# A two-layer hybrid decoder trunk on one core: a new order of the paired output tiles, and new limits in the emission planner

## The chip, the cores and the metric

The kernel runs on one core of a Trainium2 chip. The metric is device time in microseconds (us) of one execution; lower is better. Engines are named as in the profile: PE is TensorE's matmul and PEld its weight load, DVE is VectorE, ACT is ScalarE, POOL is GpSimd, SP is SyncE, which issues most of the DMAs. L468 is line 468 of the kernel before. "Tile" alone means a weight tile.

## The reference

One inference step of two layers, for 256 prompt tokens and 8 single-token samples (264 columns in all, model width 1024), all in float32:

```
x = LN(a*x + 0.5*swiglu(x))                      # FFN 0, inner width 2048
x = LN(a*x + mix(x) @ wo)
x = LN(a*x + 0.5*swiglu(x))                      # FFN 1
x = LN(a*x + sigmoid(x @ pe_gate) * (p @ pe_proj))

mix = sigmoid(m1)*(norm(o_ret)*silu(rg)) @ w_ret_out      # retention, 4 heads
    + sigmoid(m2)*(rms(o_ssm*silu(z)) * nw) @ w_ssm_out   # SSD, 16 heads, rms over 2 groups of 512
    + sigmoid(m3)*(rms(o_gdn)*nw*silu(gz)) @ w_gdn_out    # gated delta rule, 8 heads
```

Each of the three branches is a linear recurrence with a state per head. For the prompt it is computed in chunks from a zero state; the gated delta rule needs the inverse of a unit triangular 64x64 matrix per chunk and head. For each of the 8 samples one step is taken from a given state, 512 KB for each branch, sample and layer, and the updated state is written back: 48 states are updated.

## The kernel before

**Dense products.** Activations are stored transposed, 128 channels by 264 columns, as a high and a low part (`xh`, `xl`) whose sum is the float32 value; weights are split in the same way while they stream in. A weight tile is 128x1024 numbers, 512 KB. SP fetches it into `raw`, ACT copies it to the high part `whi` (L444), DVE subtracts to get the low part `wlo` (L344), and PE makes 24 matmuls of it (L468): 8 hi·xh, 8 hi·xl, 8 lo·xh. There are 239 such tiles in each layer, in a fixed order: 48 of FFN 0, 125 of the mix's inputs and branch outputs with the branches' gates between them, 8 of `wo`, 48 of FFN 1, 2 of `pe_proj`, 8 of `pe_gate`. In the mix the order is: inputs for retention (`ret`), SSD (`ssm`), `rg`; then the 8 output tiles `ro` of retention with the gate tiles `m1`; `gq`, `gv`, `mz`; SSD's output `so` with `m2`; `gz`; the delta rule's output `go` with `m3`; `wo`. The program line for DVE instructions is always L344, for ACT L444, for ACT with a running sum L442, for ACT's table loads L450, for PE L468 and its transposes L473, since a helper records them; they are told apart by their tiles.

**Prefetch.** `stream(upto)` (L562) emits the DMA and the ACT copy of the tiles up to a number; `stream_lo()` (L582) emits the DVE subtractions still owed. High and low parts live in a ring of 3; further ones, and all states and scratch of the branches, share 29 slots.

**The planner.** Emission order is set by the program itself, which keeps an estimated clock for each engine (class `Clocks`). Recurrences, sample readouts and state updates are generators ("tasks"): between weight tiles `pump()` (L668) lets a task emit its next step if the task's inputs are ready by the estimated clocks and ACT and DVE are less than a limit behind PE (`slack`, L662). A step that yields 1 was marked `easy` (L659) and may be emitted even when they are further behind; only the inverse of the triangular matrix (31 steps of two DVE instructions on `t<-inv,ub` and `ub<-ub,t`) yields 1. `drain()` (L701) and `force()` (L682) run tasks to their end at once, where their result is needed. `Clocks.dma` (L318) books a DMA at 358 bytes per ns plus a lag of 950 ns, after which what was loaded counts as ready. The state updates (`updates`) issue a state's load only if the estimated DMA queue ends before PE's clock plus a limit: `SPARE` (500) where no other task is left, `SPARE2` (-500) otherwise.

**Branch outputs.** For each of `ro`, `so`, `go`, `wo` the first two tiles are done as a pair (`two`, L745), because the branch's result `y` (split in `yh`, `yl`) comes late: first inner tiles 0 to 6 for both, then inner tile 7. The gate tiles before them (`rg`, `mz`, `gz`) multiply into the branch result one by one if its recurrence is done, or else are kept in slots (`z`) and multiplied together in `finish()` (L1361), which also drains the tasks. For SSD the function `mz` (L1375) also squares the product (ACT) and hands a closure `sq` to `late` (L1406): `DSQ` tiles later PE adds the square up with a matmul against ones, and after the eighth DVE scales and splits the result for `so`.

Of the kernel before, what the change touches and what calls it, by code (L numbers as in the profile page):

```python
# [12 lines left out]
AF = mybir.ActivationFunctionType  # L13
# [6 lines left out]
NB = 8  # L20
# [28 lines left out]
MORE_F = 4  # L49
MORE_ROOM = 0  # L50
AHEAD = 3
SPARE = 500.0
SPARE2 = -500.0
BACKLOG = 3000.0
BACKLOG_0 = 3000.0
BACKLOG_1 = 6000.0
LEAD2 = 4
HOLD = 2
DSQ = 1
NJ = 7  # L60
NN = 4
NS = 2
# [1 line left out]
UROOM = 5  # L64
UROOM_F = 4
# [168 lines left out]
class Clocks:  # L234
# [83 lines left out]
    def dma(self, key, out, in_, counts=True):  # L318
        n = 4.0
        for d in out.shape:  # L320
            n *= d
        t = self.run(key, 450.0 if key == "SP" else 1200.0, [out], [in_], False)
        t = self.at["DMA"] = max(self.at["DMA"], t) + n / 358.0
        self.note("DMA", t + 950.0, [(self.region(in_), False), (self.region(out), True)], counts)
        return t + 950.0


class Eng:
# [19 lines left out]
class Trunk:  # L348
    def __init__(self, ctx, tc, io, depth):
        self.tc, self.nc, self.io, self.depth = tc, tc.nc, io, depth  # L350
        nc = self.nc
        self.ck = Clocks()
        self.at = self.ck.at
        self.V = Eng(self, "DVE", nc.vector, 70.0, 1.05)
        self.G = Eng(self, "POOL", nc.gpsimd, 300.0, 1.55)
        self.SY = Eng(self, "SP", nc.sync, 0.0, 0.0)
        self.PE = nc.tensor
        self.ready = {}
        self.cp = ctx.enter_context(tc.tile_pool(name="cp", bufs=1))
        self.wp = ctx.enter_context(tc.tile_pool(name="wp", bufs=1))  # L360
        self.bp = ctx.enter_context(tc.tile_pool(name="bp", bufs=1))
        self.sp = ctx.enter_context(tc.tile_pool(name="sp", bufs=1))
        self.mp = ctx.enter_context(tc.tile_pool(name="mp", bufs=4, space=bass.MemoryType.PSUM))
        self.pp = ctx.enter_context(tc.tile_pool(name="pp", bufs=4, space=bass.MemoryType.PSUM))
        self.uid = 0
        self.live = 0
        self.freed = [0.0] * NSLOT
        self.peak = 0
        self.banks = 4
        self.aset = None  # L370
        self.tasks = []
        self.prio = {}
        self.easy = {}
        self.late = []
        self.total = depth * NCH
        self.wpos = self.fpos = 0
        self.raw = {}
        self.x = []
        self.wt = {}
        self.half = []  # L380
        self.more, self.ramp, self.wring, self.wslots = 0, None, [], {}
        self.res = RES
        self.hold = False
        self.ln_s = None
        self.xf = None
        self.keep = False
        self.unbiased = {}
# [261 lines left out]
    def step(self, t):  # L649

        self.ck.last = 0.0
        self.ready_at = max(self.at["PE"], self.at["DVE"])
        try:
            r = next(t)
        except StopIteration:
            self.tasks.remove(t)
            return True
        self.ready[t] = 0.0 if r == 2 else self.ck.last - (3000.0 if r else 0.0)
        self.easy[t] = r == 1  # L659
        return r != 0  # L660

    def slack(self, t):  # L662
# [5 lines left out]
    def pump(self):  # L668

        stuck = set()  # L670
        while True:
            behind = max(self.at["ACT"], self.at["DVE"]) - self.at["PE"]
            for t in self.tasks:
                if t not in stuck and self.ready.get(t, 0.0) <= self.at["PE"] and \
                        (behind < self.slack(t) or self.easy.get(t)):
                    break
            else:
                break
            if not self.step(t):
                stuck.add(t)  # L680
# [63 lines left out]

    def two(self, idx, xs):  # L745

        self.stream(idx + 3)
        self.use(idx + 1)
        ps = [self.mmtile()[:, :T] for _ in range(2)]
        for js in (range(7), (7,)):  # L750
            for j in js:
                for g in range(2):
                    for k in range(2):
                        self.mm(ps[g], self.wt[idx + g][k][:, j, :], xs[j][0], start=j == 0 and k == 0, stop=False)
            for j in js:
                for g in range(2):
                    self.mm(ps[g], self.wt[idx + g][0][:, j, :], xs[j][1], start=False, stop=j == 7)
        for g in range(2):
            self.used(idx + g)
        self.stream(idx + 4)  # L760
        return ps
# [303 lines left out]
    def pe_gate(self, idx, final):  # L1065
        wait, last = [], []

        def product(m, t):
            p = self.t4(self.prj[m // 4])[:, m % 4, :]
            self.stt(p, t, 1.0, p, ADD, MUL)  # L1070
            wait.append((m, p))

        def gate(m, ps, b, sc):
            t = self.t264()
            self.act(t, ps, AF.Tanh, scale=0.5 * sc, bias=b)
            if m == MORE_P:
                self.ramp = 0
            if m == 7:
                self.table(AF.Ln)
            if last:  # L1080
                product(*last.pop())
            last.append((m, t))
            if m == 7:
                product(*last.pop())
            if m == ALG_P:
                self.ln_begin(3, final, False)
            while m >= ALG_P and wait:
                ks = wait[:GN]
                del wait[:GN]
                for k, q in ks:  # L1090
                    self.resid(k, q)
                self.ln_add(*ks, delay=GD)
                if m < 7:
                    break
        idx = self.run(idx, 8, self.x, gate, 2, ALG_P, lambda i: True)
        self.free(*self.prj)
        self.drop()
        return idx
# [39 lines left out]
    def mix(self, idx, prev):  # L1138
        nc, V, G = self.nc, self.V, self.G
        l = self.l  # L1140
# [286 lines left out]
        convs = 28  # L1427
        for g, i in MIX[13:]:
            out = {"m2": "so", "m3": "go"}.get(g, g) if i >= LEAD2 - 2 else g
            if out in end and out not in src:  # L1430
                src[out] = end[out]()
            if g == "wo" and i == 0:
                self.free(*mixed)
                self.ln_begin(1)
                self.ramp = MORE_W
            xs = ym if g == "wo" else src[g][0] if g in src else self.x
            if i < 2 and g in ("ro", "so", "go", "wo"):
                if i == 0:
                    for e, ps in enumerate(self.two(idx, xs)):
                        do[g](e, ps)  # L1440
                        self.after()
                        self.pump()
                    idx += 2
                continue
            idx = self.run(idx, 1, xs, lambda _, ps, *a: do[g](i, ps, *a))
            convs -= g in ("ssm", "gq", "gv")
            if convs == 0:
                self.store(self.io["cso"][l], cs.rearrange("p t b -> p (t b)"), self.G)
                convs = -1
# [206 lines left out]
    def updates(self, l, todo):  # L1656

        for kind in range(3):
            while kind not in todo:
                yield 0  # L1660
            rows, decay, update = todo[kind]
            q, n = [], 0
            while n < NB or q:
                did = False
                for e in q:
                    b, S, R, k, t = e
                    if self.at["PE"] < t or self.hold and k < 2:
                        continue
                    if k == 2:
                        self.store(self.io["sts"][l, kind, b], S[0][:, 0:1024])  # L1670
                        self.free(S[0])
                        q.remove(e)
                    elif k == 1:
                        update(b, S[0], R[0])
                        self.free(R[0])
                        e[3:] = 2, self.ck.last
                    else:
                        decay(b, S[0])
                        e[3:] = 1, max(self.ck.last, R[1])
                    did = True  # L1680
                    break
                if not did and n < NB and not self.hold and self.room((UROOM_F if len(self.tasks) == 1 else UROOM) - self.res) and self.idle_dma(SPARE if len(self.tasks) == 1 else SPARE2):
                    S, R = self.ld_state(l, kind, n), self.ld_row(rows, n)
                    q.append([n, S, R, 0, S[1]])
                    n += 1
                    did = True
                yield (2 if did else 0)
# [824 lines left out]
```

## Time and profile before

| | before |
|---|---|
| runs of the kernel before | 1784.69, 1784.53, 1779.51 us (median 1784.53) |
| the profiled execution's own time | 1778.85 us |
| its span | 1777.1 us |
| mean granted TensorE clock | 0.984 of full speed |
| PE busy | 1679.2 us, 94% |
| DVE busy | 1300.5 us, 73% |
| ACT busy | 1033.8 us, 58% |
| data moved | 373.14 MB, 210 GB/s on average |

The span runs from the first to the last instruction; the execution's own time has 1.8 us more around it. Busy shares are averages over stages; the idle time of PE is read place by place in the timelines, with the engine that released it. "PEclk" is the granted TensorE clock, 1.0 for 2.4 GHz and 0.5 for 1.2 GHz. A matmul starts while the one before it drains, so busy times of single matmuls overlap.

### The profile page before, as it was taken

Reading aid. Unit: us, or ns where it says so; the run is one execution under the profiler, and the core shown is the slowest. Engines: PE = TensorE matmul, PEld = TensorE weight load, DVE = VectorE, ACT = ScalarE, POOL = GpSimd, SP = SyncE. Lnnn points to the kernel's source line nnn. Section 1 sums busy time; section 2 is a strip of 40 time slices with the busy share of each in tenths; the row PEclk is TensorE's granted clock in tenths of the full one; section 3 lists DMA queues with packets and bytes.
Section 4 is the critical chain, followed back from the end, with each engine's and each line's share of the span. In section 5 each row is a group of like instructions: output and inputs, shape, how many; then the busy total and the mean of one; then the engine's idle time right before and its main releaser. Section 6 shows DMA issues by size and latency. Waiting matters only on the chain.

```text
span 1777.1 us, 35137 instructions
## 1 busy us (share of the span) xinstructions
PE 1679.2 (94%) x14026; PEld 1592.1 (90%) x14026; DVE 1300.5 (73%) x2554; ACT 1033.8 (58%) x1918; POOL 58.6 (3%) x60
## 2 busy tenths in 40 slices
PE   8999999899989999999899999998999899999997
PEld 8999998779889898999799999987798898989996
DVE  5566858958767788777875678598586677887767
ACT  5455665347754345676764556654477544457766
POOL 0000011000000100000000000100000000000000
PEclk9999999899999999999999999998999999999999
DMA  9663557387537885598446635573774378846871
GB/s 322 179 204 125 162 193 261 107 279 243 159 101 255 313 278 195 204 337 283 151 128 183 209 123 166 200 247 115 254 253 145 114 269 321 278 158 240 324 275 45
DMA packets 129492, 373.14 MB, mean 210 GB/s; under 512 B 24032, under 2 KB 40544, under 8 KB 129328
## 3 DMA queue, kind: packets, MB, share of 16 engines
q1 hardware_dynamic: 127664, 365.13, 61.2%
q0 software_dynamic: 1664, 5.77, 0.8%
q8 instruction: 110, 1.80, 0.4%
q14 instruction: 54, 0.44, 0.1%
HBM read 334.73 MB, written 36.12 MB: 209 GB/s over the span
## 4 chain that ended last, share of the span: by engine, by line
PE 58%; DVE 22%; ACT 11%; DMA 5%; issue 3%; SPq 0%; ACTq 0%; DVEq 0%
PE mm L468 49%; PE b L468 8%; DVE wlo L344 8%; DMA S<-sti 4%; ACT whi L444 3%; DVE t L344 2%; DVE y L344 2%; ACT L450 2%; DVE S L344 2%; ACT t L444 2%; PE b L473 1%; DVE xl L344 1%; DMA raw<-w 1%; DVE gk L344 1%; DVE gv L344 1%
## 5 line engine op out<-in xcount | busy, mean ns | idle before, releaser
L444 ACT ACTIVATE whi<-raw 128x1024 fp32r<-128x1024 f32 x478 | 502.2, 1056 | 398.5 <-PE mm L468 277.2
L468 PE MATMUL mm<-xh,whi 128*128 128x264 f32 x2464 | 627.3, 290 | 16.9 <-ACT xh L444 7.6
L344 DVE TENSOR_TENSOR wlo<-raw,whi 128x1024 fp32r<-128x1024 f32 x478 | 577.8, 1219 | 67.8 <-ACT whi L444 66.7
L468 PE MATMUL mm<-xl,whi 128*128 128x264 f32 x2464 | 618.1, 286 | 2.6 <-DVE xl L344 2.3
L468 PEld LDWEIGHTS mm<-xh,whi 128*128 128x128 f32 x2464 | 466.3, 189 | 32.8 <-issue 12.5
L468 PEld LDWEIGHTS mm<-xl,whi 128*128 128x128 f32 x2464 | 466.3, 189 | 6.6 <-DVE xl L344 4.1
L468 PE MATMUL mm<-xh,wlo 128*128 128x264 f32 x2464 | 351.3, 285 | 6.6 <-DVE wlo L344 6.5
L468 PEld LDWEIGHTS mm<-xh,wlo 128*128 128x128 f32 x2464 | 320.7, 189 | 8.7 <-DVE wlo L344 8.4
L468 PE MATMUL mm<-yh,whi 128*128 128x264 f32 x512 | 136.6, 299 | 4.8 <-ACT yh L444 4.8
L468 PE MATMUL mm<-hh,whi 128*128 128x264 f32 x512 | 128.4, 287 | 0.0
L468 PE MATMUL mm<-hl,whi 128*128 128x264 f32 x512 | 127.1, 284 | 0.0
L468 PE MATMUL mm<-yl,whi 128*128 128x264 f32 x512 | 113.5, 284 | 0.0
L468 PEld LDWEIGHTS mm<-yh,whi 128*128 128x128 f32 x512 | 101.4, 198 | 10.8 <-ACT yh L444 6.2
L468 PE MATMUL mm<-yh,wlo 128*128 128x264 f32 x512 | 93.7, 295 | 14.7 <-DVE wlo L344 14.7
L468 PEld LDWEIGHTS mm<-hh,whi 128*128 128x128 f32 x512 | 96.4, 188 | 5.1 <-issue 5.1
L468 PEld LDWEIGHTS mm<-hl,whi 128*128 128x128 f32 x512 | 96.4, 188 | 0.0
L468 PEld LDWEIGHTS mm<-yh,wlo 128*128 128x128 f32 x512 | 79.2, 198 | 16.3 <-DVE wlo L344 16.3
L468 PEld LDWEIGHTS mm<-yl,whi 128*128 128x128 f32 x512 | 88.9, 188 | 0.0
L468 PE MATMUL mm<-gh,whi 128*128 128x266 f32 x304 | 82.3, 292 | 0.0
L468 PE MATMUL mm<-gl,whi 128*128 128x266 f32 x304 | 80.4, 286 | 0.0
L468 PE MATMUL mm<-hh,wlo 128*128 128x264 f32 x512 | 72.6, 284 | 0.9 <-DVE wlo L344 0.9
L468 PEld LDWEIGHTS mm<-hh,wlo 128*128 128x128 f32 x512 | 66.3, 188 | 1.1 <-DVE wlo L344 1.1
(322 smaller groups left out, 2241.3 us busy)
## 6 DMA issues: line engine op xcount, KB each, us to landing
raw<-w SPq DMA_DIRECT2D x478, 512.0 KB, 4.3
S<-sti SPq DMA_DIRECT2D x96, 512.0 KB, 6.7
sts<-S SPq DMA_DIRECT2D x48, 512.0 KB, 5.6
vB<-rowsr SPq DMA_DIRECT2D x16, 512.0 KB, 8.2
vB<-rowss SPq DMA_DIRECT2D x16, 512.0 KB, 7.5
vB<-rowsg SPq DMA_DIRECT2D x16, 512.0 KB, 7.8
dm<-mt SPq DMA_DIRECT2D x4, 512.0 KB, 6.3
T<-imgt SPq DMA_DIRECT2D x4, 512.0 KB, 8.0
```

Of the source, the lines that this page charges most:

```text
L344: return f(out, *a, **k)
L444: self.nc.scalar.activation(out, in_, func, bias=bias, scale=scale)
L450: self.nc.scalar.preload_act_table_set(self.aset)
L468: self.PE.matmul(out, lhsT, rhs, start=start, stop=stop, **kw)
L473: self.PE.transpose(out, in_, self.ident[:k, :k])
```

## The change

- `two()` now does, for inner tiles 0 to 6 and then for 7, all hi·yh products, then all hi·yl, then all lo·yh. Before, hi·yh and lo·yh alternated for each inner tile, and hi·yl came last. It asks for one tile ahead (`idx + 1`) instead of three; and ahead of the branch's `finish()` two tiles and their low parts are now asked for.
- The exception for `easy` steps is gone: inverse steps obey the same limit as all others.
- `DSQ` is 2 instead of 1. The lag of a DMA in the planner is 2200 instead of 950. `SPARE` is 3000 instead of 500, `SPARE2` 500 in the first layer and 700 in the last instead of -500.
- In `pe_gate` the table load for `Ln` stands behind the last products and residual sums instead of before them.

```diff
-SPARE = 500.0
-SPARE2 = -500.0
+DMA_LAG = 2200.0
+SPARE = 3000.0
+SPARE2 = 500.0, 700.0
...
-DSQ = 1
+DSQ = 2
...
-        self.note("DMA", t + 950.0, [(self.region(in_), False), (self.region(out), True)], counts)
-        return t + 950.0
+        self.note("DMA", t + DMA_LAG, [(self.region(in_), False), (self.region(out), True)], counts)
+        return t + DMA_LAG
...
-        self.easy[t] = r == 1
...
-                        (behind < self.slack(t) or self.easy.get(t)):
+                        behind < self.slack(t):
...
     def two(self, idx, xs):
 
-        self.stream(idx + 3)
+        self.stream(idx + 1)
         self.use(idx + 1)
         ps = [self.mmtile()[:, :T] for _ in range(2)]
         for js in (range(7), (7,)):
-            for j in js:
-                for g in range(2):
-                    for k in range(2):
-                        self.mm(ps[g], self.wt[idx + g][k][:, j, :], xs[j][0], start=j == 0 and k == 0, stop=False)
-            for j in js:
-                for g in range(2):
-                    self.mm(ps[g], self.wt[idx + g][0][:, j, :], xs[j][1], start=False, stop=j == 7)
+            for k, e in ((0, 0), (0, 1), (1, 0)):
+                for j in js:
+                    for g in range(2):
+                        self.mm(ps[g], self.wt[idx + g][k][:, j, :], xs[j][e], start=j == 0 and k + e == 0, stop=j == 7 and k == 1)
...
-            if m == 7:
-                self.table(AF.Ln)
             if last:
                 product(*last.pop())
...
+            if m == 7:
+                self.table(AF.Ln)
         idx = self.run(idx, 8, self.x, gate, 2, ALG_P, lambda i: True)
...
         for g, i in MIX[13:]:
             out = {"m2": "so", "m3": "go"}.get(g, g) if i >= LEAD2 - 2 else g
+            if g in ("ro", "so", "go", "wo") and i == 0:
+                self.stream(idx + 2)
+                self.stream_lo()
             if out in end and out not in src:
                 src[out] = end[out]()
...
+                alone = len(self.tasks) == 1
...
```

Since the planner sets the order, these lines move instructions in many places. Three of them follow; lines of the changed kernel are one higher than those of the kernel before. `mm` is a PSUM tile of a dense product, `b` any other PSUM tile, `c` the constants (ones and identity among them), `sx` SSD's result, `t` scratch; the number behind a name tells tiles apart.

PE at SSD's square sums in layer 0, around a tile of `mz`. Before:

```order
L468 MATMUL mm_5929<-xh_1895,wlo_5829 128x264 x4
L468 MATMUL mm_5929<-xh_1896,wlo_5829 128x264 x4
L468 MATMUL b_5868<-t_5901,c 128x264
L473 MATMUL b_5966<-c,gv_5469 128x128 x4
L473 MATMUL b_5972<-c,gv_5469 128x128 x4
L468 MATMUL mm_5978<-xh_1895,whi_5855 128x264
```

And of the changed kernel, after the last tile of `mz` and its successor:

```order
L468 MATMUL mm_6158<-xh_1895,wlo_6058 128x264 x4
L468 MATMUL mm_6158<-xh_1896,wlo_6058 128x264 x4
L468 MATMUL b_6097<-z_5753,c 128x264 x4
L468 MATMUL b_6106<-z_5943,c 128x264 x3
L468 MATMUL b_6106<-t_6088,c 128x264
L468 MATMUL mm_6230<-xh_1895,whi_6084 128x264
```

Before, one square sum (`b_5868<-t_5901,c`) stood behind each tile; now all eight stand in one row, two tiles behind the last tile of `mz`, of squares that were made together from kept tiles.

DVE at the pair of `so` in layer 0 (`rms_6073` and `t_6268` are the two factors of the norm, `n` the norm of the delta rule's result). Before:

```order
L344 TENSOR_TENSOR wlo_6235<-raw_6116,whi_6210 128x1024
L344 SCALAR_TENSOR_TENSOR sx_3379<-sx_3379,pv_129,rms_6073 128x264 x4
L344 TENSOR_TENSOR yl_5864<-sx_3379,yh_5862 128x264 x4
L344 SCALAR_TENSOR_TENSOR sx_3573<-sx_3573,pv_129,t_6268 128x264 x4
L344 TENSOR_TENSOR yl_5865<-sx_3573,yh_5863 128x264 x4
L344 TENSOR_TENSOR wlo_6299<-raw_6166,whi_6261 128x1024
L344 TENSOR_TENSOR wlo_6332<-raw_6212,whi_6325 128x1024
L344 TENSOR_TENSOR n_6364<-n_6364,gq_5299 128x2x4
L344 TENSOR_SCALAR n_6365<-n_6364 128x8
L344 TENSOR_TENSOR wlo_6378<-raw_6263,whi_6358 128x1024
```

And of the changed kernel:

```order
L345 TENSOR_TENSOR wlo_6126<-raw_5980,whi_6084 128x1024
L345 TENSOR_TENSOR wlo_6159<-raw_6032,whi_6152 128x1024
L345 SCALAR_TENSOR_TENSOR sx_3375<-sx_3375,pv_129,rms_6194 128x264 x4
L345 TENSOR_TENSOR yl_6093<-sx_3375,yh_6091 128x264 x4
L345 SCALAR_TENSOR_TENSOR sx_3588<-sx_3588,pv_129,t_6200 128x264 x4
L345 TENSOR_TENSOR yl_6094<-sx_3588,yh_6092 128x264 x4
L345 TENSOR_TENSOR wlo_6231<-raw_6086,whi_6185 128x1024
L345 TENSOR_TENSOR t_6271<-b_6265,gk_2771 128x512
L345 COPY gsm_1833<-gv_5573 128x32
L345 TENSOR_TENSOR wlo_6278<-raw_6154,whi_6257 128x1024
```

The two instructions on `n`, which need ACT's sums of squares of the delta rule, no longer stand between the low parts of the pair's weights.

PE at the pair of `ro` in layer 0 (`sb`, `sx`, `sd`, `vt`, `ktd` belong to SSD's recurrence and readouts). Before:

```order
L473 MATMUL b_4203<-c,sd_4144 64x128
L468 MATMUL b_4209<-sd_4145,c 128x16
L468 MATMUL b_4217<-vt_3055,ktd_3054 128x256
L468 MATMUL b_4217<-vt_3056,ktd_3054 128x256
...
L468 MATMUL mm_4266<-yh_4230,whi_4047 128x264
L468 MATMUL mm_4266<-yh_4230,wlo_4058 128x264
L468 MATMUL mm_4267<-yh_4230,whi_4084 128x264
L468 MATMUL mm_4267<-yh_4230,wlo_4095 128x264
```

And of the changed kernel:

```order
L468 MATMUL mm_4131<-xh_1895,wlo_4047 128x264 x4
L468 MATMUL mm_4131<-xh_1896,wlo_4047 128x264 x4
L468 MATMUL mm_4195<-yh_4165,whi_4073 128x264
L468 MATMUL mm_4196<-yh_4165,whi_4120 128x264
...
L468 MATMUL mm_4195<-yl_4167,whi_4073 128x264
L468 MATMUL mm_4196<-yl_4167,whi_4120 128x264
...
L468 MATMUL mm_4195<-yh_4165,wlo_4094 128x264
L468 MATMUL mm_4196<-yh_4165,wlo_4132 128x264
```

SSD's steps no longer stand between the last tile of `rg` and the pair, and in the pair the low parts (`wlo`) come last.

## Rows read from the trace of the kernel before

**Rows 1.** The page: span; busy time of each engine, share, instructions.

```profile
span 1777.1 us, 35137 instructions
...
PE 1679.2 (94%) x14026; PEld 1592.1 (90%) x14026; DVE 1300.5 (73%) x2554; ACT 1033.8 (58%) x1918; POOL 58.6 (3%) x60
```

**Rows 2.** The chain of waits, first FFN: start us, us, what.

```profile
8.83 116.88 PE mm L468 x951
```

**Rows 3.** All waits of PE: engine, line, waited for: us in total, times, longest.

```profile
PE mm L468 <- DVE wlo L344: 22.1, 15, 4.8
PE b L468 <- ACT t L444: 10.1, 7, 3.7
PE b L468 <- DMA S<-sti: 9.9, 11, 1.9
```

**Rows 4.** Timeline of PE at the square sums, layer 0; in brackets idle time before.

```profile
480.95 1.25 PE L468 MATMUL b<-t,c 128*128 128x264 f32 x2 [3.71 <-ACT t L444]
```

**Rows 5.** Timeline of DVE at the same place.

```profile
478.42 1.22 DVE L344 TENSOR_TENSOR wlo<-raw,whi 128x1024 fp32r<-128x1024 f32 x1
...
480.01 0.43 DVE L344 TENSOR_TENSOR sx<-sx,t 128x264 f32<-128x264 f32 x1
```

**Rows 6.** Stretches: length, busy PE, PEld, DVE, ACT, POOL, PEclk, DMA share, GB/s.

```profile
349.00:354.00 5.00, 4.93 (x28) 4.93 (x29) 5.00 (x15) 3.45 (x9) 0.00 (x0) 0.66 0.21 85
481.00:487.00 6.00, 6.00 (x27) 5.53 (x28) 2.58 (x4) 5.01 (x11) 0.00 (x0) 0.55 0.73 224
534.00:538.00 4.00, 3.44 (x17) 3.45 (x18) 2.86 (x4) 1.13 (x2) 2.02 (x1) 0.54 0.49 169
1231.00:1238.00 7.00, 6.71 (x33) 6.72 (x33) 7.00 (x17) 3.66 (x9) 0.00 (x0) 0.54 0.19 76
```

**Rows 7.** Timeline of PE at the so pair, layer 0.

```profile
527.86 1.23 PE L468 MATMUL mm<-xh,wlo 128*128 128x264 f32 x8 [1.98 <-DVE wlo L344]
...
534.55 0.59 PE L468 MATMUL mm<-yh,wlo 128*128 128x264 f32 x1 [4.76 <-DVE wlo L344]
```

**Rows 8.** Timeline of DVE at the so pair, layer 0.

```profile
520.60 1.71 DVE L344 SCALAR_TENSOR_TENSOR sx<-sx,pv,rms 128x264 f32<-128x264 f32 x4 [3.53 <-ACT rms L444]
...
526.59 2.35 DVE L344 TENSOR_TENSOR wlo<-raw,whi 128x1024 fp32r<-128x1024 f32 x2
532.99 0.17 DVE L344 TENSOR_TENSOR n<-n,gq 128x8 f32<-128x8 f32 x1 [4.05 <-ACT t L442]
...
533.27 1.23 DVE L344 TENSOR_TENSOR wlo<-raw,whi 128x1024 fp32r<-128x1024 f32 x1
```

**Rows 9.** Timeline of PE at the ro pair, layer 0.

```profile
340.42 0.39 PE L473 MATMUL b<-c,sd 128*64 128x128 f32 x1 [2.73 <-DVE sd L344]
...
342.91 3.76 PE L468 MATMUL b<-vt,ktd 128*128 128x256 f32 x8 [1.12 <-DVE xd L344]
349.07 0.39 PE L468 MATMUL mm<-yh,whi 128*128 128x264 f32 x1 [2.40 <-ACT yh L444]
```

**Rows 10.** Timeline of DVE at the ro pair, layer 0.

```profile
337.90 0.39 DVE L344 TENSOR_TENSOR t<-inv,ub 64x231 f32<-64x231 f32 x1
...
348.03 0.18 DVE L344 TENSOR_TENSOR ub<-ub,t 64x31 f32<-64x31 f32 x1
348.14 1.45 DVE L344 TENSOR_TENSOR z<-z,ro 128x264 f32<-128x264 f32 x4
```

**Rows 11.** ScalarE table loads, whole span: count, ns, first and last start.

```profile
L450 ACT ACT_TABLE_LOAD  x48: 1283/1283/1283, 13.8 to 1762.0; - x48
```

**Rows 12.** DVE by line and shape: one piece of a state update.

```profile
L344 DVE SCALAR_TENSOR_TENSOR S<-vB,gsm,S 128x128 f32<-128x128 f32 x128 | 35.0, 346 | 0.2 <-ACT S L444 0.2
```

**Rows 13.** Span and mean granted TensorE clock.

```profile
core 0: 1777.1 us, clock 0.984
```

**Rows 14.** The page: DMA issues of state tiles: count, KB, us to landing.

```profile
S<-sti SPq DMA_DIRECT2D x96, 512.0 KB, 6.7
```

**Rows 15.** The page: FFN matmuls that wait for a low part.

```profile
L468 PE MATMUL mm<-hh,wlo 128*128 128x264 f32 x512 | 72.6, 284 | 0.9 <-DVE wlo L344 0.9
```

More of the change, by code (lines that the diff above doesn't have):

```diff
@@ L372, in __init__ @@
         self.prio = {}
-        self.easy = {}
         self.late = []
@@ L1681, in updates @@
                     break
-                if not did and n < NB and not self.hold and self.room((UROOM_F if len(self.tasks) == 1 else UROOM) - self.res) and self.idle_dma(SPARE if len(self.tasks) == 1 else SPARE2):
+                alone = len(self.tasks) == 1
+                if not did and n < NB and not self.hold and self.room((UROOM_F if alone else UROOM) - self.res) and self.idle_dma(SPARE if alone else SPARE2[l == self.depth - 1]):
                     S, R = self.ld_state(l, kind, n), self.ld_row(rows, n)
```

## The prediction

> **What bounds the kernel now.** I read the page first. PE is busy for 94% of the span, DVE for 73%, ACT for 58% [rows 1]. So PE's own matmuls set most of the time, and the change alters none of them: it only reorders. In the chain of waits a long stretch of the first FFN shows the price of a dense matmul with nothing in its way: 951 in 116.88 us, 0.1229 us each [rows 2], so a tile of 24 takes 2.95 us. What reordering can give back is PE's idle time and the time in which its clock is low. The list of PE's waits says what ends the idle time [rows 3]: low parts of weights (22.1 us, 15 times), a square or similar from ACT before a product in `b` (10.1 us), and sample states on their way from memory (9.9 us). The timelines then say where. The mean granted clock is 0.984 [rows 13], so the low clock is a small share of the span, but it stands right behind these waits, as the stretches show [rows 6].
>
> The sum below starts from the profiled execution's own time, 1778.85 us; the median of the runs, 1784.53, is 5.7 us higher.
>
> **A. SSD's square sums.** Now PE waits 3.71 us for ACT's square at the first sums [rows 4]. DVE shows why: that square's product is queued behind a low part [rows 5]. Behind the wait PE works at a clock of 0.55 for 6 us [rows 6], which costs 6 x 0.45 = 2.7 us. Layer 1 repeats it: 2 x (3.71 + 2.7) = 12.8 us. In the changed order the eight sums stand in one row two tiles after the last of `mz`. Their squares need eight products of 0.43 us and at most one low part of 1.22 us on DVE [rows 5], 4.7 us, with ACT a step behind. Two tiles give 2 x 2.95 = 5.9 us of cover. It is just enough, so I take 12 of the 12.8 us. If the cover fails by one tile's length, the wait is back and 7 us are left; that is the lower bound.
>
> **B. The pair of `so`.** Two waits, 1.98 and 4.76 us [rows 7]. The first is for a low part that DVE makes only after scaling and splitting SSD's result; the second for one that stands on DVE behind the instructions on `n`, which wait 4.05 us for ACT's eight squares of the delta rule [rows 8]. Then PE runs 4 us at 0.54 [rows 6], costing 1.8 us. Twice: 2 x (1.98 + 4.76 + 1.8) = 17.1 us. The changed order has no `n` there, and the pair uses its low parts last. What is late next is the result itself: from the sums on, DVE waits 3.53 us for ACT's roots and then works 1.71 + 1.46 + 1.70 + 1.45 = 6.3 us [rows 8] to scale and split. The sums now come after the second gate tile of `m2`, so that only the remaining two tiles, 5.9 us, cover it; the second half's scaled values are there at 3.53 + 1.71 + 1.46 + 1.70 = 8.4 us, and the pair needs them after eight matmuls, at 5.9 + 1.0 = 6.9. So a new wait of 1.5 us, and 2.9 if the split of the last half counts too. I take 2.5 for each layer: 17.1 - 5 = 12.1 us.
>
> **C. The pair of `ro`.** Before it PE drains SSD's readouts and waits 2.73, 1.12 and 2.40 us [rows 9], since DVE is working through inverse steps meanwhile (22 instructions from 0.39 down to 0.18 us between the first and last row of [rows 10], some 6.6 us), and only then multiplies the gate into the result. With the low clock behind it (5 us at 0.66, 1.7 us; in layer 1 7 us at 0.54, 3.2 us [rows 6]) that is 2 x 6.25 + 4.9 = 17.4 us. In the new order PE goes from the last `rg` tile straight to the pair. But it then needs a gated and split result that DVE makes in pieces: four gate products in 1.45 us, 0.36 each [rows 10]. Seven products and four splits take 11 x 0.36 = 4.0 us, whereas the first 14 matmuls of the pair last 1.7 us; the tanh of the last gate and DVE's own backlog, 0 to 3 us, come ahead. I charge 5 us per layer, between 3.5 and 6.5: 17.4 - 10 = 7.4 us.
>
> **D. The pairs of `go` and `wo`.** Of the 22.1 us of waits for low parts [rows 3], 2 x 6.74 are in B. The other 8.6 us lie in 13 places; the new order of the pair touches those at `go` and `wo`. I take 3 us, bounds 0 and 8.6.
>
> **E. Sample readouts.** PE waits 9.9 us in 11 places for states [rows 3], because the planner counts a state as there earlier than the trace has it: the median from issue to landing is 6.7 us [rows 14]. The larger lag puts the matmuls later. I take half, 5 us; bounds 0 and 9.9.
>
> **F. What is put off.** Removing the exception for inverse steps and adding lag moves SSD's and the delta rule's work later: SSD's readouts end some 20 tiles later, and one half of the delta rule about 4 to 9. This work has the same instructions, so nothing is added on DVE, but it can meet a new place where PE needs it at once. No row shows this. The nearest is the drain at `ro`, 6.25 us and its clock. Nothing of it, or two of it per layer, are the ends: 0 and 24 us. I take one for each layer, 12 us, as the same tasks now run among tiles that also need DVE for gates.
>
> **G. Table loads.** The changed order has 52 instead of 48 loads of 1.283 us [rows 11]: 5.1 us of ACT. ACT is idle for 42% of the span [rows 1], and I cost them at nothing; without that cover 5.1 us is the bound. The moved `Ln` load in `pe_gate` stands behind the same matmuls either way: 0, give or take 0.3 us.
>
> **H. State updates.** The new limits put updates some 17 to 20 tiles later, into FFN 1, and of the first layer's last ones into the second layer's FFN 0. Their arithmetic is unchanged and lies beside dense tiles. The very last stands among the final gate tiles: eight DVE pieces of 0.346 us [rows 12], 2.8 us, beside a tail in which DVE is on the path. I take 1 us; bounds 0 and 2.8.
>
> **Sum.** 12 + 12.1 + 7.4 + 3 + 5 = 39.5 gained, 12 + 0 + 1 lost, 26.5 us in all: 1752.3 against the profiled execution's own 1778.85. Since the median of three lies 5.7 us above that execution, I add half of it: **1755 us**.
>
> **Rivals.** *The clock comes back everywhere, and nothing new waits* (F is 0). The sum is then 38.5 us, 1740 us, and where the low stretches vanish whole it is lower still. For it: low stretches stand right behind the waits removed. Against: F moves work, it does not delete it. The Trainium skill, "TensorE: Matmul & The Clock Gate", section "Terms", prices a throttled clock as the throttled time times the share of pulses withheld; by that rule a mean of 0.984 would be worth 0.016 x 1777 = 28 us in all, against the 13.9 us that A to C take from the stretches, and the sum would end up to 14 us lower. The rows do not contradict the rule; they say that I counted only stretches where PE was also busy. This case spans 1722 to 1735 beyond my forecast's own lower end; chance 0.12.
>
> *The new waits eat the gain.* Each deferred group meets a pair: two such waits per layer with their clock, F = 24 us, and `ro` at 6.5, A at 7: 39.5 - 5 - 3 - 24 - 1 = 6.5 us left, 1772 to 1790. For it: DVE has little room in the mix, and a wait of 4.05 us for ACT's squares [rows 8] stands somewhere in any order. Chance 0.16.
>
> *Slower: the weights lose their lead.* Updates that run 17 to 20 tiles later hold slots (a state and its row, two of 29, for each in flight) that `stream` would use for weights ahead, and their 512 KB loads stand before weights on SP's queue. A tile whose low part is late costs about 0.9 us, which is what the FFN's matmuls waited in all [rows 15]. About 120 tiles lie in the moved stretches. The gain of 39.5 us is gone when 44 tiles pay this, beyond which the kernel is slower; all of them would cost 108 us. Against: that row has 0.9 us over 512 matmuls, and updates already ran beside the FFN's tiles in this trace. The Trainium skill, "DMA: Bandwidth & Descriptors", section "Queues, rings and completion order", says that each DMA engine consumes descriptors in ring order, which would let a state load delay the weights behind it; the row on the FFN's waits shows that so far they had enough lead. Chance 0.10, over 1790 us.
>
> *The change does nothing* would need PE's order unchanged at A to C; the printed orders show otherwise, so it has no share.
>
> **How the numbers follow.** A measurement of this kernel tells about 0.3% (5.35 us) from no change: faster means under 1779.2, slower over 1789.9. My forecast's own case, 1735 to 1772, has 0.62. Faster: 0.62 + 0.12 + half of the second rival, 0.08 = 0.82. Within 0.3%: the other half, 0.08. Slower: 0.10. The range from 1728 to 1782 leaves out the slower rival, some 0.05 at the upper end of the second and 0.05 below.
>
> **What would show it.** Right: no 3.71 us wait at the square sums, none of 4.76 us at `so`, no inverse steps between the last `rg` tile and the pair of `ro`, a mean clock above 0.984, and PE's total of waits for low parts well below 22.1 us. B and C are wrong if the pairs wait over 3 and 6.5 us for `yh` or `yl`. E is wrong if waits for `S<-sti` stay near 9.9 us. The prediction as a whole is wrong if waits for `raw` or `wlo` appear in the FFN stages, or if the same waits turn up around `gz` and `go`.

## The result, and the profile after

The changed kernel took 1751.16 us (median; 1749.24 to 1752.27), the kernel before 1782.68 us beside it: a ratio of 0.9824, 95% interval 0.9804 to 0.9844. A second comparison gave 0.9809 (0.9789 to 0.983). The forecast was 1755 us within 1728 to 1782, and faster. In the profiled executions the span fell from 1777.1 to 1749.6 us, 27.5 us; that is less than the 31.5 us between the medians, since the profiled execution of the kernel before (1778.85 us) is the fastest on record for it.

The page of the changed kernel, part 1, and its mean clock:

```profile
span 1749.6 us, 35165 instructions
...
PE 1673.8 (96%) x14026; PEld 1591.0 (91%) x14026; DVE 1297.7 (74%) x2554; ACT 1040.8 (59%) x1922; POOL 57.9 (3%) x60
```

```profile
core 0: 1749.6 us, clock 0.990
```


PE is busy 5.4 us less than before [rows 1], although it makes the same 14026 matmuls; the mean clock rose from 0.984 [rows 13] to 0.990. Over all executions with a recorded clock it is 0.975 to 0.984 for the kernel before and 0.988 to 0.991 for the changed one. The list of PE's waits (engine, line, waited for: us in total, times, longest) shows where its idle time went:

```profile
PE mm L468 <- ACT yh L444: 11.4, 4, 6.2
PE mm L468 <- DVE t L345: 8.2, 10, 2.2
...
PE b L468 <- DVE y L345: 7.2, 7, 2.0
PE mm L468 <- DVE wlo L345: 5.5, 9, 1.4
PE b L468 <- DVE t L345: 5.0, 4, 1.9
PE b L473 <- DVE t L345: 4.4, 4, 1.7
PE b L473 <- ACT dt L444: 3.4, 2, 1.7
PE b L468 <- ACT t L444: 2.4, 7, 1.1
```


Against [rows 3], waits for low parts fell from 22.1 to 5.5 us, those for ACT's `t` from 10.1 to 2.4, and those for sample states (9.9 us) are gone from the list. Two classes are new (transposes `b L473` behind DVE's `t`, 4.4 us, and ACT's `dt`, 3.4 us), and waits for `yh` (4.8 us before), `y` (4.8), and DVE's `t` (7.0 in dense products, 3.1 in `b L468`) are up. These four before:

```profile
PE mm L468 <- DVE t L344: 7.0, 10, 1.0
...
PE b L468 <- DVE y L344: 4.8, 5, 2.0
PE mm L468 <- ACT yh L444: 4.8, 2, 2.4
PE b L468 <- DVE t L344: 3.1, 2, 1.6
```


The same places as in [rows 7, 9], on PE's timeline; first the pair of `ro` in layers 0 and 1, then the pair of `so` in layer 0:

```profile
342.19 1.73 PE L468 MATMUL mm<-yh,whi 128*128 128x264 f32 x8 [3.59 <-ACT yh L444]
344.94 1.69 PE L468 MATMUL mm<-yh,whi 128*128 128x264 f32 x6 [1.02 <-ACT yh L444]
```

```profile
1213.94 2.13 PE L468 MATMUL mm<-yh,whi 128*128 128x264 f32 x8 [6.16 <-ACT yh L444]
1216.69 1.69 PE L468 MATMUL mm<-yh,whi 128*128 128x264 f32 x6 [0.62 <-ACT yh L444]
```

```profile
512.19 1.85 PE L468 MATMUL mm<-yh,whi 128*128 128x264 f32 x13 [0.49 <-ACT whi L444]
...
516.33 1.85 PE L468 MATMUL mm<-yh,wlo 128*128 128x264 f32 x13 [0.47 <-DVE wlo L345]
```


At `so` 6.74 us of waiting became 0.96 (in layer 1 6.80 became 0.84). At `ro` the three waits of the drain became two for the split result, 4.61 us in layer 0 and 6.78 in layer 1. The stretches (length, busy PE, PEld, DVE, ACT, POOL, PEclk, DMA share, GB/s) to set beside [rows 6]:

```profile
342.00:349.00 7.00, 5.80 (x26) 5.36 (x27) 5.97 (x16) 2.62 (x8) 0.00 (x0) 0.60 0.26 77
499.00:505.00 6.00, 6.00 (x38) 5.48 (x37) 2.65 (x3) 4.07 (x7) 0.00 (x0) 1.00 0.53 161
512.00:518.00 6.00, 5.34 (x41) 5.13 (x42) 4.29 (x6) 3.53 (x6) 0.00 (x0) 1.00 0.41 99
1213.00:1220.00 7.00, 5.43 (x23) 5.13 (x24) 5.59 (x17) 2.91 (x8) 0.00 (x0) 0.50 0.30 88
```


In layer 0 the clock stays at 1.00 at the square sums and at `so`; it is still low (0.60, 0.50) at both pairs of `ro`.

From the trace's records of PE, the length of each stage (from the first matmul of its first weight tile to that of the next stage) and PE's idle time in it, summed over its gaps (us; layer 0, layer 1):

| tiles | length before | length now | idle before | idle now |
|---|---|---|---|---|
| FFN 0 to `ssm` | 298.9, 306.4 | 299.1, 311.0 | 5.7, 10.5 | 5.4, 11.0 |
| `rg`, `ro`, `gq` | 137.6, 139.2 | 132.3, 134.7 | 9.5, 10.2 | 8.6, 11.4 |
| `gv`, `mz`, `so`, `gz` | 173.8, 173.8 | 161.0, 160.4 | 14.2, 14.3 | 3.5, 2.2 |
| `m3`, `go`, `wo` | 76.6, 76.5 | 76.8, 77.5 | 2.5, 2.6 | 1.9, 2.6 |
| FFN 1, `pe_proj`, `pe_gate` | 187.7, 189.5 | 188.2, 191.7 | 5.8, 6.1 | 5.8, 6.8 |

From the start of the last matmul both have 11.1 us. Idle time fell by 22 us over the span, from 81 to 59, and by 22.8 us between `gv` and `gz` alone; elsewhere it came out even. The second layer's first stage takes 4.6 us back. At its start DVE's timeline shows a state update in the middle of the layer norm:

```profile
875.34 2.12 DVE L345 TENSOR_TENSOR y<-y,b 128x264 f32<-128x264 f32 x6
877.38 2.19 DVE L345 SCALAR_TENSOR_TENSOR S<-vB,gsm,S 128x128 f32<-128x128 f32 x8
879.49 0.22 DVE L345 COPY n<-mm 128x2 f32<-128x2 f32 x2
```

### The profile page after: what moved, and what is told of

Its sections match the earlier page's. It is cut to its first block, busy times and chain, and to the rows that moved or that the text cites. A ratio compares the mean times of both kernels' runs of the same rounds, so it can differ in the third digit from the quotient of the medians.

```text
span 1749.6 us, 35165 instructions
## 1 busy us (share of the span) xinstructions
PE 1673.8 (96%) x14026; PEld 1591.0 (91%) x14026; DVE 1297.7 (74%) x2554; ACT 1040.8 (59%) x1922; POOL 57.9 (3%) x60
## 4 chain that ended last, share of the span: by engine, by line
PE 63%; DVE 23%; ACT 10%; issue 3%; DMA 1%; POOL 0%; ACTq 0%; DVEq 0%; POOLq 0%
PE mm L468 54%; PE b L468 8%; DVE wlo L345 8%; DVE t L345 3%; DVE y L345 3%; ACT whi L444 2%; DVE S L345 2%; ACT L450 2%; ACT t L444 1%; PE b L473 1%; DVE sx L345 1%; DVE xl L345 1%; DVE ub L345 1%; DVE gq L345 1%; DMA raw<-w 1%
## 5 line engine op out<-in xcount | busy, mean ns | idle before, releaser
L468 PE MATMUL mm<-xh,whi 128*128 128x264 f32 x2464 | 627.1, 290 | 18.1 <-DVE t L345 8.2
L468 PE MATMUL mm<-xl,whi 128*128 128x264 f32 x2464 | 618.8, 286 | 2.6 <-DVE xl L345 2.3
L468 PEld LDWEIGHTS mm<-xh,whi 128*128 128x128 f32 x2464 | 466.4, 189 | 31.8 <-issue 13.5
L468 PEld LDWEIGHTS mm<-xl,whi 128*128 128x128 f32 x2464 | 466.5, 189 | 6.0 <-DVE xl L345 4.1
L468 PE MATMUL mm<-xh,wlo 128*128 128x264 f32 x2464 | 354.3, 286 | 4.1 <-DVE wlo L345 4.0
L468 PEld LDWEIGHTS mm<-xh,wlo 128*128 128x128 f32 x2464 | 324.1, 190 | 5.5 <-DVE wlo L345 5.5
L468 PE MATMUL mm<-yh,whi 128*128 128x264 f32 x512 | 120.0, 297 | 12.4 <-ACT yh L444 11.4
L468 PE MATMUL mm<-hh,whi 128*128 128x264 f32 x512 | 128.7, 287 | 0.0
L468 PE MATMUL mm<-hl,whi 128*128 128x264 f32 x512 | 127.5, 284 | 0.0
L468 PE MATMUL mm<-yl,whi 128*128 128x264 f32 x512 | 116.3, 291 | 0.0
L468 PEld LDWEIGHTS mm<-yh,whi 128*128 128x128 f32 x512 | 91.4, 194 | 17.2 <-ACT yh L444 12.4
L468 PEld LDWEIGHTS mm<-hh,whi 128*128 128x128 f32 x512 | 96.3, 188 | 5.1 <-issue 5.1
L468 PEld LDWEIGHTS mm<-hl,whi 128*128 128x128 f32 x512 | 96.4, 188 | 0.0
L468 PEld LDWEIGHTS mm<-yl,whi 128*128 128x128 f32 x512 | 91.6, 195 | 0.0
L468 PE MATMUL mm<-gh,whi 128*128 128x266 f32 x304 | 82.4, 293 | 0.0
L468 PE MATMUL mm<-gl,whi 128*128 128x266 f32 x304 | 80.5, 286 | 0.0
L468 PE MATMUL mm<-yh,wlo 128*128 128x264 f32 x512 | 73.9, 286 | 1.5 <-DVE wlo L345 1.5
L468 PE MATMUL mm<-hh,wlo 128*128 128x264 f32 x512 | 72.7, 284 | 0.0
L468 PEld LDWEIGHTS mm<-yh,wlo 128*128 128x128 f32 x512 | 67.2, 189 | 2.3 <-DVE wlo L345 2.3
```

The source lines that it names most:

```text
L468: self.PE.matmul(out, lhsT, rhs, start=start, stop=stop, **kw)
```

## The experiments

Twelve runs were made, in three groups, each beside the kernel before, whose median was 1784.38, 1787.87 and 1784.67 us in them. So ratios to it are compared; the changed kernel's is 0.981 to 0.982. Theory 1 is that of the prediction: each part of the change removes the wait of its own place.

**The pair's order, undone.**

```diff
-        self.stream(idx + 1)
+        self.stream(idx + 3)
...
-            for k, e in ((0, 0), (0, 1), (1, 0)):
-                for j in js:
-                    for g in range(2):
-                        self.mm(ps[g], self.wt[idx + g][k][:, j, :], xs[j][e], start=j == 0 and k + e == 0, stop=j == 7 and k == 1)
+            for j in js:
+                for g in range(2):
+                    for k in range(2):
+                        self.mm(ps[g], self.wt[idx + g][k][:, j, :], xs[j][0], start=j == 0 and k == 0, stop=False)
+            for j in js:
+                for g in range(2):
+                    self.mm(ps[g], self.wt[idx + g][0][:, j, :], xs[j][1], start=False, stop=j == 7)
...
-            if g in ("ro", "so", "go", "wo") and i == 0:
-                self.stream(idx + 2)
-                self.stream_lo()
```

> The changed kernel with the old order in the pairs (high and low parts alternating) and without the two tiles asked for ahead of the pair; all other parts stay. Theory 1 (each part of the change removes the wait of its own place): the waits for low parts at the pairs of go and wo come back, 6.1 us over both layers as in the kernel before, and low parts are wanted earlier at ro and so: 1756 to 1764 us. Rival (the pair's order is worth nothing once the tasks stand elsewhere): 1749 to 1753 us.

Measured: 1776.63 us, 0.9951 (0.9934 to 0.9968). This one part is worth 1.3%, some 23 us, far more than theory 1 gave it. Against the changed kernel's trace PE is idle for 12 us more (71 for 59) and busy for 15 us more (1688.7 for 1673.8) with the same matmuls, at a mean clock of 0.979. Its waits of PE, and its timeline at `so` and at `go`:

```profile
PE mm L468 <- DVE wlo L345: 22.7, 17, 3.5
```

```profile
515.21 0.39 PE L468 MATMUL mm<-yh,wlo 128*128 128x264 f32 x1 [3.05 <-DVE wlo L345]
...
516.34 0.59 PE L468 MATMUL mm<-yh,wlo 128*128 128x264 f32 x1 [0.62 <-DVE wlo L345]
```

```profile
616.16 0.39 PE L468 MATMUL mm<-yh,wlo 128*128 128x264 f32 x1 [0.47 <-DVE wlo L345]
...
618.43 0.59 PE L468 MATMUL mm<-yh,wlo 128*128 128x264 f32 x1 [1.76 <-DVE wlo L345]
```


The waits for low parts are back at 22.7 us, those of the kernel before. At `so` PE waits 3.67 us for low parts, although in this run the instructions on `n` come at 546 us on DVE, 30 us behind the pair. With the old order the second matmul already needs a low part, which DVE makes from 513.94 us on, behind the scaling and splitting; with the new one 28 matmuls lie ahead of the first.

**The inverse's exception, back.**

```diff
+        self.easy[t] = r == 1
...
-                        behind < self.slack(t):
+                        (behind < self.slack(t) or self.easy.get(t)):
```

> The changed kernel with the exception for inverse steps back. The printed order has 105 and 85 SSD matmuls between the last rg tile and the pair of ro again. Theory 1: the drain at ro returns with its waits of over 6 us in each layer, minus the waits for yh that the changed kernel has there: 1756 to 1766 us. Rival (11 to 13 inverse steps of two short DVE instructions are too little to matter): 1749 to 1754 us.

Measured: 1767.59 us, 0.9901 (0.9884 to 0.9917), 1.6 us above theory 1's range; taken by its ratio, just inside it. PE at the pair of `ro` in layer 0 (lines one higher):

```profile
338.31 0.83 PE L474 MATMUL b<-c,sx 128*128 128x128 f32 x4 [4.50 <-DVE t L345]
...
340.89 0.69 PE L474 MATMUL b<-c,t 128*128 128x128 f32 x2 [1.29 <-DVE xd L345]
```


SSD's work stands ahead of the pair again and waits for DVE, which works through inverse steps among other things meanwhile.

**Square sums one tile later, undone.** `DSQ = 1` in the changed kernel.

> The changed kernel with square sums one tile after their gate tile instead of two. All eight still stand in one row, now one tile earlier, with 2.95 us of cover against 4.7 us of DVE work. Theory 1: a wait of 1.8 to 3.7 us at the sums returns in each layer, with a stretch at the low clock behind it: 1755 to 1763 us. Rival (the squares are ready anyway, since kept tiles are gated early): 1750 to 1753 us.

Measured: 1749.06 us, 0.9803 (0.9786 to 0.9819). The rival holds: in this kernel the second tile of cover is not needed. The timelines of DVE and then of ACT in the changed kernel have the last products and the squares in a row:

```profile
495.00 0.43 DVE L345 SCALAR_TENSOR_TENSOR t<-t,mm 128x264 f32<-128x264 f32 x1 [1.11 <-ACT t L444]
495.35 2.48 DVE L345 TENSOR_TENSOR sx<-sx,z 128x264 f32<-128x264 f32 x7
```

```profile
495.81 2.48 ACT L444 ACTIVATE z<-sx 128x264 f32<-128x264 f32 x7 [0.84 <-DVE sx L345]
498.21 0.42 ACT L444 ACTIVATE t<-sx 128x264 f32<-128x264 f32 x1
```

All are ready at 498.63 us, 3.6 us after DVE takes up the last gate's product; nothing on DVE comes between. With `DSQ = 1` the same rows stand 0.5 us later, and PE takes up the sums while ACT still makes squares:

```profile
496.30 2.49 ACT L444 ACTIVATE z<-sx 128x264 f32<-128x264 f32 x7 [0.84 <-DVE sx L345]
```

```profile
498.67 3.28 PE L468 MATMUL b<-z,c 128*128 128x264 f32 x14
```

PE starts without all the squares being there, and ACT makes the next ones (0.34 us each) faster than PE adds them up (0.45 us each). That seven tiles are kept and gated in one go is not the only way to lose the wait: in the run with the old pair the products come one by one at this place (497.87 and 500.48 us on DVE), with `DSQ = 2`, and no wait for ACT's `t` is longer than 1.15 us.

**The DMA lag, undone.** `DMA_LAG = 950.0` in the changed kernel.

> The changed kernel with the planner's DMA lag at 950 again. Theory 1: the waits for sample states return, up to 9.9 us in all, and the rest of the gain stays: 1755 to 1765 us. Rival (the lag is the lever that puts SSD's work out of the way, and the other parts follow from it): 1770 us or more.

Measured: 1762.56 us, 0.9874 (0.9859 to 0.9889), in theory 1's range. The waits for states return:

```profile
PE b L468 <- DMA S<-sti: 7.6, 5, 3.0
```


**The limits for updates, undone.** `SPARE = 500.0`, `SPARE2 = -500.0, -500.0` in the changed kernel.

> The changed kernel with the old limits for loading states for updates. The printed order puts the last layer's last five updates behind the last weight tile, and the first layer's last five into the next layer's FFN 0, clear of the layer boundary. Theory 1: the new limits only make good what the larger lag delays; without them five updates of at least 2.8 us of DVE each, with their loads and stores, lie bare at the end: 1760 to 1785 us. Rival (updates lie beside dense work wherever they are): 1747 to 1754 us.

Measured: 1770.78 us, 0.9906 (0.989 to 0.9923), in theory 1's range. In the profiled execution the cost is all at the end: the last matmul starts at 1736.4 us, in the changed kernel at 1738.5, and then 34 us pass instead of 11. DVE there:

```profile
1743.17 2.19 DVE L345 SCALAR_TENSOR_TENSOR S<-vB,gsm,S 128x128 f32<-128x128 f32 x8
1752.26 2.19 DVE L345 SCALAR_TENSOR_TENSOR S<-vB,gsm,S 128x128 f32<-128x128 f32 x8 [6.91 <-DMA vB<-rowsg]
1755.00 2.19 DVE L345 SCALAR_TENSOR_TENSOR S<-vB,gsm,S 128x128 f32<-128x128 f32 x8 [0.55 <-ACT S L444]
1757.49 2.19 DVE L345 SCALAR_TENSOR_TENSOR S<-vB,gsm,S 128x128 f32<-128x128 f32 x8 [0.30 <-ACT S L444]
```


**The Ln load, undone.**

```diff
-            if m == 7:
-                self.table(AF.Ln)
         idx = self.run(idx, 8, self.x, gate, 2, ALG_P, lambda i: True)
```

with the two lines back ahead of the last products.

> The changed kernel with the table load for Ln back ahead of the last products in the gate of the layer input. Theory 1 (the load stands behind the same matmuls either way): 1751 us, within 0.3. Rival, from the trace of the changed kernel, where DVE waits 2.64 us for ACT at the layer boundary instead of 1.78 us: the later load costs 0.9 us in each layer, and this kernel gives 1749 to 1750 us.

Measured: 1750.43 us, 0.9791 (0.9776 to 0.9806). The interval overlaps with the changed kernel's; theory and rival are less than 2 us apart, and this doesn't tell them apart.

**The new pair alone, in the kernel before.**

> The kernel before with the new order in the pairs and the two tiles ahead of them alone. Theory 1: the second wait at so (4.76 us) and those at go and wo go, 15.6 us over both layers, against new waits for the split result at so of about 2.5 us each; the square sums and the drain at ro stay; two updates fall behind the last tile, 5 us: 1768 to 1778 us. Rival (all of the gain is in the pairs): 1755 us or less.

Measured: 1764.62 us, 0.9872 (0.9853 to 0.9891). By its ratio it is 23 us faster, more than theory 1's 10 to 20 and less than the rival's. Waits for low parts are nearly gone:

```profile
PE mm L468 <- DVE wlo L344: 3.9, 9, 1.0
```


**The lag alone, in the kernel before.**

> The kernel before with a DMA lag of 2200 in the planner alone. The printed order has no SSD matmuls left between the last rg tile and the pair of ro, but four updates behind the last tile. Theory 1: the waits for states go (9.9 us), part of the drain at ro goes (5 to 10 us), and the bare updates take back 10 us or more: 1770 to 1782 us. Rival (the lag alone carries the gain): 1760 us or less.

Measured: 1802.89 us, 1.0089 (1.0069 to 1.0108): slower, which neither theory had. Its low parts are later than before, and from the start of the last matmul 20 us pass instead of 11.1, with an update among them (columns as above):

```profile
PE mm L468 <- DVE wlo L344: 30.5, 15, 6.0
```

```profile
1779.50:1800.20 20.70, 0.70 (x2) 0.00 (x0) 8.77 (x26) 7.26 (x20) 0.00 (x0) 0.50 0.41 154
```


The lag takes most of the waits for states away (1.2 us are left) and hands more back at the old pairs and behind the last tile. In the changed kernel it pays, as the run with 950 shows, with the new pair and the new limits both there; no run shows which of the two it needs.

**The changed kernel once more, and three variants, timed together.** The repetition:

> The changed kernel itself, as the base of the three others of this call: 1749 to 1753 us, 0.982 of the kernel before.

Measured: 1750.68 us, 0.9809 (0.9789 to 0.983).

Without the tiles asked for ahead of the pair, the order kept:

```diff
-            if g in ("ro", "so", "go", "wo") and i == 0:
-                self.stream(idx + 2)
-                self.stream_lo()
```

> The changed kernel without the three lines that ask for two tiles and their low parts ahead of a branch's finish; the pair keeps its new order. Theory 1 (the order of the matmuls carries the pair's gain, since 28 of them, 3.4 us, now lie ahead of the first low part): at most 5 us slower than the changed kernel. Rival (the tiles asked for ahead carry it): 15 us slower or more.

Measured: 1750.74 us, 0.9808 (0.9785 to 0.983), no difference. So the order of the matmuls carries the pair's gain, unless asking for one tile instead of three inside the pair does: the run with the old pair undid both, and no run separates them.

Without an update between the layers:

```diff
-                if not did and n < NB and not self.hold and self.room(
+                if not did and n < NB and not self.hold and not (self.shut and l == 0) and self.room(
...
         for m in range(4, 8):
             p = self.mmtile()
+            self.shut = ln == 2 and m >= 5
```

and `self.shut = False` at the end of `pe_gate`.

> The changed kernel, but the first layer issues no more loads for state updates from the sixth output tile of FFN 1 to the end of the layer, so that no update is forced between the layers; three updates then run inside the next FFN 0, beside its dense tiles. Theory 1 (the 8 DVE pieces, 2.2 us, in the middle of the layer norm cost their own length and the low clock behind it): 2 to 4 us faster than the changed kernel, all of it in the first 48 tiles of the second layer. Rival (the place was hidden, or the updates cost as much where they go): no change, within 1 us.

Measured: 1747.72 us, 0.9792 (0.9771 to 0.9814). The medians differ by 3.0 us as theory 1 has it, but the intervals overlap, and in the profiled executions the second layer's FFN 0 is only 1.8 us shorter (154.9 against 156.7). DVE now goes on without the update:

```profile
878.48 2.12 DVE L345 TENSOR_TENSOR y<-y,b 128x264 f32<-128x264 f32 x6
880.51 0.22 DVE L345 COPY n<-mm 128x2 f32<-128x2 f32 x2
```


Three of the variants in one:

> The changed kernel with square sums one tile after their gate tile, the Ln load at its old place and no update forced between the layers. If the three small differences add up (2 us, 1 us, 2 to 4 us): 1743 to 1747 us, 4 to 8 us faster than the changed kernel. If each was chance or is taken back by the other: the same as the changed kernel, within 2 us.

Measured: 1747.17 us, 0.9787 (0.9766 to 0.9807). It is no better than the one before it: the small differences don't add up. Both have lower medians than the changed kernel, and neither is shown to beat it.

## Why the prediction was right, and where it was not

The time and the sign came out, 1751 for 1755. The mechanism was right in the main: waits and low clock went at the places named. But several terms were off and made good for each other, so that the time is this near is in part luck.

**A, the square sums (12).** Right in size: waits for ACT's `t` fell by 7.7 us, and the clock at the sums went from 0.55 [rows 6] to 1.00: with 2.7 us for the clock in each layer, 13 us. Its reason was wrong. I made it rest on two tiles of cover, "just enough", for all eight products; in the run with one tile PE begins while squares are still being made, and nothing is lost.

**B, the pair of `so` (12.1).** The waits fell by 5.8 and 6.0 us and the 1.8 us of low clock are gone in layer 0; with the same in layer 1 that is 15 us. Two steps failed. I put the second wait down to "the instructions on `n`" alone; the run with the old pair has them elsewhere and waits 3.67 of the 6.74 us all the same, so by that run `n` made up 3 us at most, and the pair's order is needed for the rest. And the new wait for the split result, 2.5 us, did not come. I had taken DVE's 3.53 us of waiting for the time from the sums to the roots. The sums, DVE's scaling of the two halves and the pair stand so in the changed kernel:

```profile
504.24 0.61 PE L468 MATMUL b<-t,c 128*128 128x264 f32 x2
...
511.42 0.28 PE L468 MATMUL mm<-yh,whi 128*128 128x264 f32 x1
```

```profile
506.04 1.71 DVE L345 SCALAR_TENSOR_TENSOR sx<-sx,pv,rms 128x264 f32<-128x264 f32 x4 [4.39 <-ACT rms L444]
...
509.03 1.70 DVE L345 SCALAR_TENSOR_TENSOR sx<-sx,pv,t 128x264 f32<-128x264 f32 x4
```

DVE begins 1.2 us behind the end of the sums, and the second half is scaled 5.9 us behind it instead of 8.4, before the pair begins.

**C, the pair of `ro` (7.4).** Mis-sized. The new waits, 4.61 and 6.78 us, are near the 3.5 to 6.5 that I charged; the second is over the 6.5 that I named as a sign of being wrong. Two steps failed, both about the low clock. I left out the low clock behind the new waits: by the stretches above at most 7 x 0.40 and 7 x 0.50, 6.3 us. And I left out the low clock inside the old drain: the eight products `b<-vt,ktd` take 3.76 us there [rows 9], against 1.89 us a little earlier in the same trace, so 1.9 us more were lost in each layer before:

```profile
334.46 1.89 PE L468 MATMUL b<-vt,ktd 128*128 128x256 f32 x8
```

So the waits went from 12.5 to 11.4 us and the low clock from some 8.7 to 6.3: C gave about 3.5 us. PE's idle time in the whole stage hardly changed, since waits of F stand in it. The stage is 5 us shorter in each layer all the same: it also has 22 fewer `b` matmuls (505 for 527), most of which stand in the next one (403 for 387).

**D, `go` and `wo` (3).** Right in size: by PE's timelines the waits for low parts in this stage fell from 5.2 to 2.4 us over both layers, and at the pairs themselves to 0.6. (The 8.6 us outside of B lie in 11 places, not 13.) Idle time in the stage fell by only 0.6 us, as waits for `y` in the norm behind `wo` took their place.

**E, readouts (5).** All 9.9 us of waits for states went, and 7.6 us come back with the old lag. **F, what is put off (-12).** By the list of waits, the two new classes and the growth of those for `y` and `t` come to 4.4 + 3.4 + 2.4 + 1.2 + 1.9 = 13.3 us. But 1.2 us of this stand at the start of the second layer and 1.0 in the last stage, which belong to H:

```profile
890.06 0.36 PE L468 MATMUL mm<-xh,whi 128*128 128x264 f32 x1 [2.20 <-DVE t L345]
...
1735.18 0.63 PE L468 MATMUL b<-y,c 128*32 128x264 f32 x2 [1.26 <-DVE y L345]
```

Some 11 us are left. This was the largest guess, from the nearest row alone. Its size held and its form did not: I had one drain like that at `ro` for each layer, and there came waits of at most 1.9 us in many places.

**G, table loads (0).** Four more (52), and nothing shows a cost. **H, state updates (-1).** Mis-sized: 4.6 us are lost up to `ssm` in the second layer and 2.2 us in its last stage. I looked for the cost among the last gate tiles alone; an update in the layer norm between the layers was not in the sum. Taking it out gave back 1.8 to 3 us, so it is a part of that loss and not all.

By these rows A to E gained some 44 us where I had 39.5, and F and H took some 18 where I had 13: 26 of the 27.5 us between the profiled spans, and 26.5 forecast. Of the signs of being wrong, besides C's in layer 1, two came, both small: a wait of 0.32 us for a low part in FFN 0 of the second layer, and 1.8 us of such waits at gate tiles around `go`.

Of the rivals, "the clock comes back everywhere" failed at `ro`. The rule of the Trainium skill, "TensorE: Matmul & The Clock Gate", section "Terms", would price the rise of the mean clock at 0.006 x 1777 = 11 us, an estimate. The trace shows half of it: PE's busy time, for the same matmuls, fell by 5.4 us. The stretches at the sums and at `so` alone gave 2 x 2.7 + 2 x 1.8 = 9.0, and new low stretches took some of it back. "The weights lose their lead" did not happen in the changed kernel, where 5.5 us of waits for low parts are left; the run with the lag alone shows that it could have, with 30.5 us.

The parts don't add. Undone one at a time they cost, by the ratios against 0.982, some 23 us (pair), 15 (exception), 10 (lag) and 15 (limits): 63 us against a gain of 32. The pair's order is the largest part either way, 23 us undone and 23 us alone, where B and D gave it 15. With the larger lag and the old limits five updates land behind the last tile. What stays open: whether the lag needs the new pair or only the new limits, which of the edits makes the square sums cheap (the run with the new pair alone already waits less there, 5.2 us for ACT's `t` in all), and whether the Ln load costs 1 us.

## What to carry to other kernels

Where a product is split in parts that become ready at different times, issue first all matmuls that need only the early parts: 28 matmuls of cover removed nearly all waits for late weights, and asking for the weights earlier added nothing. A planner's estimate is worth no more than its neighbours allow: the truer DMA lag alone made the kernel 0.9% slower, with 9 us more behind the last tile and later low parts at the old pairs. Before costing deferred work at nothing, look for the places with no cover (a norm between layers, the tail) and see which of it can land there.

## What was not expected of the hardware

Waits of about half a microsecond left the granted clock at 1.00 (0.49 and 0.47 us at `so`), while those of 3.59 and 6.16 us at `ro` were followed by stretches at 0.60 and 0.50. In between, the same wait can go either way. At the end of `gq` PE waits 1.68 us for ACT's `dt` in layer 0 and 1.74 us in layer 1, and the next 4 us of the same work ran at 1.00 and at 0.57, with 33 matmuls and with 23 (columns as above):

```profile
437.00:441.00 4.00, 4.00 (x33) 4.00 (x34) 2.64 (x5) 3.70 (x8) 1.66 (x1) 1.00 0.69 255
1309.00:1313.00 4.00, 4.00 (x23) 4.00 (x22) 2.27 (x5) 2.48 (x6) 1.66 (x1) 0.57 0.66 225
```

So differences of 2 or 3 us between single executions, and mean clocks of single executions, bear little reading. The profiled run with the old pair has a lower mean clock than the profiled kernel before (0.979 for 0.984) with less idle time on PE, 71 us against 81; but over its four executions the clock is 0.979 to 0.985, and that of the kernel before beside it 0.976 to 0.981.
